# Three token-major projection groups of 512, 512 and 420 columns in place of four, with the index columns beside the chunked mixer

## The chip, the cores and the metric

The kernel runs on one core of a Trainium2 chip. The metric is the device time of the program on that core, in microseconds (us); lower is better.

## What is computed

Two layers of a decoder trunk with 512 tokens of width 1024. In each layer one input projection of the normalised tokens feeds four mixers of width 256, whose gated outputs are merged and projected back:

```
h = rmsnorm(x, g_pre)
proj = jnp.einsum('bsd,dc->bsc', h, w_in)
(a_q, a_k, a_v, a_iq, a_ik, a_iw, b_b, b_c, b_x, c_q, c_k, c_v,
 d_u, d_v, gate_paths, merge_logits) = _split_cols(proj, IN_SPLITS)
o_a = dsa_sparse_attention(rope(a_q), rope(a_k), a_v, rope(a_iq), rope(a_ik), a_iw)
o_b = short_gated_conv(b_b, b_c, b_x, conv_w, conv_b)
o_c = stick_breaking_attention(c_q, c_k, c_v)
o_d = chunked_spatial_gating(d_u, d_v, ln_g, ln_b, w_spatial, b_spatial)
z = jnp.einsum('bsnw,nwd->bsnd', stack(o_a, o_b, o_c, o_d) * silu(gate_paths), w_branch)
merged = jnp.sum(jax.nn.sigmoid(merge_logits + b_merge) * z, axis=2)
x = x + rmsnorm(merged @ w_out, g_post)
x = x + (p_i @ w_ple) * sigmoid(x @ w_ple_gate)
```

Mixer A picks, for each token, its 128 best earlier tokens by an index score (from the columns iq, ik and iw) and attends to those alone. Mixer C (stick-breaking attention) needs cq, ck and cv. Mixer D (chunked gating) normalises dv per token and mixes it inside chunks of 128 tokens.

## The kernel before

Every float32 product is made of three matmuls on TensorE (`mm3`, L267 to L271): both factors are split into a rounded half and the rest (names ending in h and l), and hh, hl and lh are summed in PSUM. A weight chunk of up to 128 x 1024 arrives by DMA as `raw`; `split_chunk` makes `wh` on ScalarE (L246) and `wl` on VectorE (L248). `cmm` uses `wh`, `wh`, `wl` as the stationary operands of the first three matmuls of a step, so `wl` is wanted by the third.

The order of work on all engines is written out by `step`, one call of which is a step of the plan here. A step emits, in this order: the ScalarE and VectorE work on results of earlier steps (`front`), the splits that are due, the work of the mixers (`back`), the selection of mixer A (`idle`); then the step's main matmuls; then any split that is due only after them (a late split); then short matmuls and transposes that the generators asked for with `yield PE`. Each engine runs its own list in that order, so what stands in one step's list on VectorE delays all that stands behind it.

In each layer the steps are: T1 (aq, ak; 512 columns, token-major), cq and ck in steps 4 to 7, CV (cv, 256 columns) in 8 and 9, T2 (av, iq, ik, iw; 420 columns) in 10 to 13, the convolution's six column steps in 14 to 19, du in 20 and 21, DV (dv, 256 columns) in 22 and 23, eight gate steps in 24 to 31 and 32 merge steps in 32 to 63. A column step or a T step has 24 matmuls; a merge step has 24 into `mg` and 6 into `z`. CV and DV go through `tpairs`: two token tiles of 256 columns share a PSUM bank and 48 matmuls make one step.

The selection (`select`, L840 and after) builds for tiles 1, 2 and 3 a score row `cur` of 256, 384 or 512 columns and then runs 16 rounds on VectorE: MAX8 finds the eight largest, MATCH_REPLACE8 strikes them out. `RATES` says how many rounds a step may emit: 1 from its start in the convolution steps, 2 from du on, 3 in the gate steps, 2 in the merge steps. In the merge steps a late split falls due in steps 35, 39, 43, 47, 51 and 55, for the first merge chunk of the very next step.

Of the kernel before, what the change touches and what calls it, by code (L numbers as in the profile page):

```python
# [12 lines left out]
F32R = mybir.dt.float32r  # L13
I32 = mybir.dt.int32
AF = mybir.ActivationFunctionType
ALU = mybir.AluOpType
# [4 lines left out]
P = 128  # L21
# [23 lines left out]
def _span(name, i=0, n=None):  # L45
    o, w = OFF[name]
    n = w if n is None else n
    return list(range(o + i, o + i + n))
# [4 lines left out]

TGROUPS = {
    "T1": _span("aq") + _span("ak"),
    "T2": _span("av") + _span("iq") + _span("ik") + _span("iw"),
    "CV": _span("cv"),
    "DV": _span("dv"),
}
CCOLS = {(n, c): _span(n, P * c, P) for n in ("cq", "ck", "bb", "bc", "bx", "du") for c in range(2)}  # L60
CCOLS.update({(f"gate{n}", c): _span("gate", W * n + P * c, P) for n in range(4) for c in range(2)})
# [1 line left out]

PAIRED = ("T1", "T2", "Y0", "Y1", "G0")


def tiles_of(cols):
# [3 lines left out]
def chunk_plan():  # L73

    plan, step = [], 0
    for l in range(L):
        here = []

        def tgroup(name, cols, steps):
            nonlocal step  # L80
            n = tiles_of(cols)
            for c in range(KT // n):
                first, last = step, step + steps - 1
                if name in PAIRED and (l, name) != (0, "T1"):
                    first, last = step + c // 2, step + c // 2 + 2
                here.append(("t", n * cols, (name, c), first, last))
            step += steps

        def ccols(*names):
            nonlocal step  # L90
            for a in names:
                here.append(("c", KT * P, a, step, step))
                step += 1

        def both(n):
            return [(n, 0), (n, 1)]

        tgroup("T1", 512, 4)
        ccols(*both("cq"), *both("ck"))
        tgroup("CV", 256, 2)  # L100
        tgroup("T2", 420, 4)
        for c in range(2):
            ccols(("bc", c), ("bx", c), ("bb", c))
        ccols(*both("du"))
        tgroup("DV", 256, 2)
        for n in MERGES:
            ccols(*both(f"gate{n}"))
        for n in MERGES:
            for h in range(2):
                here.append(("w", 1024, (n, h), step, step + 3))  # L110
                ccols(*((f"merge{n}", dt) for dt in range(4 * h, 4 * h + 4)))
        for h in range(2):
            tgroup(f"Y{h}", 512, 4)
        for h in range(2):
            here.append(("p", 1024, h, step, step))
            step += 1
            tgroup(f"G{h}", 512, 4)
        plan.append(here)
    return plan
# [34 lines left out]
QB, TB, SB, RAWB, WB, LEAD = 10, 25, 24, 3, 6, 4  # L154


STICKD, SELECT0, ATTEND0, RATES = 3, 8, 5, (1, 2, 3, 2)


START = ("s0 h0 t0 w e0 m00 s1 h1 w t1 m01 e1 s2 h2 m10,11 t2 w e2 s3 h3 m02,12,20,21 t3 w e3 "  # L160
# [20 lines left out]
def hybrid_kernel(ctx: ExitStack, tc: tile.TileContext, w, x, p_t, pos, inv_freq, rows, small, ws_t, b_sp, out):  # L181
# [12 lines left out]
    def T(name, shape=(P, 512), dt=F32):  # L194
        return tpool.tile(list(shape), dt, tag="t", name=name)
# [21 lines left out]
    def bank(name):  # L217
        return psum.tile([P, 512], F32, tag="ps", name=name)
# [40 lines left out]
    def take(n=1):  # L259
        k = state["use"]  # L260
        state["use"] += n
        for c in chunks[k:k + n]:
            assert c[3] <= state["step"] + n
        return list(range(k, k + n))
# [10 lines left out]
    def half_h(h, src, scale=None):  # L275
        if scale is None:
            A.copy(h, src)
        else:
            A.mul(h, src, scale)
# [35 lines left out]
    def step(mm=None):  # L315
        splits = list(due(False)) if mm else []
        if chained[0]:
            waiting = rounds(list(front))
            waiting += rounds(splits + back)
        else:  # L320
            waiting = rounds(front + splits + back)
        waiting += rounds(list(idle))
        if mm:
            mm()
            rounds(list(due(True)))
        while waiting:
            waiting = rounds(waiting)
        if mm:
            state["step"] += 1
# [143 lines left out]
    def heads(x):  # L473
        return x.rearrange("p (n f) -> p n f", n=4)
# [10 lines left out]
    def tmm(ps, lhs, ks, t, cols, n, kts=range(KT), cs=slice(0, 512)):  # L485
        for kt in kts:
            h, lo = halves[ks[kt // n]]
            s = slice(kt % n * cols + cs.start, kt % n * cols + min(cs.stop, cols))
            mm3(ps, lhs(kt, t), (h[:, s], lo[:, s]), kt == 0, kt == KT - 1)
# [26 lines left out]
            step(lambda: tmm(ps[:, :cols], lhs, ks, t, cols, n))  # L516
            front.append(use(t, ps))

    def tpairs(lhs, use):

        ks = take(2)
        for t in (0, 2):
            ps = bank("tp")

            def mm():
                for i in range(2):
                    tmm(ps[:, 256 * i:256 * i + 256], lhs, ks, t + i, 256, 4)

            step(mm)
            front.append(use(t, ps.rearrange("p (t f) -> p t f", t=2)))  # L530

    def ccol(use):

        k, = take()
# [76 lines left out]
    for l in range(L):  # L611
# [170 lines left out]
        sticks = [later(stick(c, b), STICKD * (2 * c + b)) for c in range(2) for b in range(2)]  # L782
        back.extend(sticks)

        def use_cv(t, ps):
            for i in range(2):
                half_h(vc[:, t + i, :, 0], heads(ps[:, i]))
            yield HOP
            for i in range(2):
                half_l(vc[:, t + i, :, 0], vc[:, t + i, :, 1], heads(ps[:, i]))  # L790

        tpairs(hlhs, use_cv)

        va = stacked("va")
        ikT = T("ikT", dt=F32R)

        def use_t2(t, ps):
            half_h(va[:, t, :, 0], heads(ps[:, 0:256]))
            iw = sm("iw", 4)
            V.tensor_scalar(iw, ps[:, 416:420], IDX_SCALE, None, op0=ALU.mult)  # L800
            iws[t] = iw
            r = T("ir")
            rope(r[:, :160], ps[:, 256:416], cos32, sin32, 5, t, "ropei")
            yield HOP
            half_l(va[:, t, :, 0], va[:, t, :, 1], heads(ps[:, 0:256]))

            sk = T("isk")[:, :P].rearrange("p (a b f) -> p a b f", a=2, b=2)
            rk = r[:, 128:160]
            rk2 = rk[:, None, :].to_broadcast([P, 2, 32])
            if t:  # L810
                sq = T("isq", (P, 4, 2, 2, 32))
                rq = r[:, :128].rearrange("p (h f) -> p h f", h=4)
                for a in range(2):
                    A.copy(sq[:, :, 0, a].bitcast(F32R), rq)
            for a in range(2):
                A.copy(sk[:, a, 0].bitcast(F32R), rk)
            yield HOP
            if t:
                for a in range(2):
                    V.tensor_tensor(sq[:, :, 1, a], rq, sq[:, :, 0, a], op=ALU.subtract)  # L820
            V.tensor_tensor(sk[:, :, 1], rk2, sk[:, :, 0], op=ALU.subtract)
            yield PE
            if t:
                tp = bank("iqtr")
                for h in range(4):
                    nc.tensor.transpose(tp[:, h * P:(h + 1) * P], sq[:, h].rearrange("p a b f -> p (a b f)"), ident)
            tk = bank("iktr")
            nc.tensor.transpose(tk[:, :P], sk.rearrange("p a b f -> p (a b f)"), ident)
            yield STEP
            if t:  # L830
                q = T("iqT", dt=F32R)
                A.copy(q, tp)
                iqT[t] = q
            V.tensor_copy(ikT[:, t * P:(t + 1) * P], tk[:, :P])

        tgroup(hlhs, 420, use_t2, 1)

        rate = {"select": 0}

        def select():  # L840

            bias[0] = bias0
            for i in range(1, NT):
                n = (i + 1) * P
                cur = T("cur")
                for h in range(4):
# [111 lines left out]
                yield STEP  # L958


        idle.append(later(select(), SELECT0))
        rate["select"] = RATES[0]
        cur = {}

        def use_bc(c, ps):
# [29 lines left out]
            A.copy(du[c], ps)  # L995
            yield STEP

        rate["select"] = RATES[1]
        for c in range(2):
            ccol(lambda ps, c=c: use_du(c, ps))  # L1000
        lnp = load(T("lnp"), bass.AP(tensor=rows.tensor, offset=rows.offset + l * 2560 + 2048, ap=[[0, P], [1, 512]]))
# [9 lines left out]
            yield HOP  # L1011
            yield from split(wsT[0], wsT[1], ws)

        def use_dv(t, ps):
            mv, r = sm("bag", 4), sm("lnr", 2)
            for i in range(2):
                st = sm("bst", 6)
                V.bn_stats(st, ps[:, i])
                V.bn_aggr(mv[:, 2 * i:2 * i + 2], st)
            yield from rstd(r, [mv.rearrange("p (t k) -> p t k", t=2)[:, :, 1]], 1)  # L1020
            yield HOP
            vf = T("vf", (P, 2, W))
            for i in range(2):
                V.tensor_scalar(vf[:, i], ps[:, i], mv[:, 2 * i:2 * i + 1], r[:, i:i + 1], op0=ALU.subtract, op1=ALU.mult)
            g, b = [lnp[:, W * i:W * i + W][:, None, :].to_broadcast([P, 2, W]) for i in range(2)]
            V.tensor_tensor(vf, vf, g, op=ALU.mult)
            V.tensor_tensor(vf, vf, b, op=ALU.add)
            yield HOP
            yield from split(vn[0][:, t:t + 2], vn[1][:, t:t + 2], vf)

        def mix():
            for c in range(2):
# [19 lines left out]
                raw[3, c] = o  # L1052

        back.append(prepare_ws())
        tpairs(hlhs, use_dv)
        back.append(later(mix(), 1))


        rate["select"] = RATES[2]

        def use_gate(n, c, ps):
            g = T("gate")
# [13 lines left out]
        for n in MERGES:  # L1076
            for c in range(2):
                ccol(lambda ps, n=n, c=c: use_gate(n, c, ps))
        rate["select"] = RATES[3]


        m, mT = {}, {}
# [219 lines left out]
```

## Time and profile before

| | |
|---|---|
| median of three runs | 1103.43 us (1102.41 to 1104.86) |
| the profiled execution | 1104.97 us |
| its span, first to last instruction | 1103.3 us |
| TensorE matmul (PE) | 1088.5 us busy, 99% |
| VectorE (DVE) | 771.8 us, 70% |
| ScalarE (ACT) | 492.3 us, 45% |
| GpSimd (POOL) | 23.0 us, 2% |
| mean granted TensorE clock | 0.997 |

The busy share of an engine is that of the whole span. TensorE is the engine that is never idle for long; another engine costs time where TensorE waits for it. Of the chain of work that ended last, the page of the profile puts 93% on TensorE and 4% on VectorE.

### The profile page before, as it was taken

What the parts mean: (1) busy time and instruction counts of PE and PEld (TensorE: products, weight loads), DVE (VectorE), ACT (ScalarE), POOL (GpSimd) and SP (SyncE); (2) the same over time, 40 slices, a digit from 0 to 9 for tenths busy, and PEclk for the clock granted to TensorE, in tenths of its full rate; (3) what the DMA queues carried; (4) which work ended last, traced back from release to release, by engine and by line L of the source; (5) the groups of instructions that cost most, each with busy time, mean ns of one, the idle gap of its engine ahead of it and who ended that gap; (6) DMA issues with size and microseconds to landing.
All of it is one profiled execution on the core that took longest, in us unless ns stands there. A gap on an engine that the chain in (4) does not pass through costs nothing.

```text
span 1103.3 us, 14018 instructions
## 1 busy us (share of the span) xinstructions
PE 1088.5 (99%) x5300; PEld 923.3 (84%) x5300; DVE 771.8 (70%) x1450; ACT 492.3 (45%) x857; POOL 23.0 (2%) x46
## 2 busy tenths in 40 slices
PE   7989999999999999999999999999999999999998
PEld 5879889888888888888788998988888888888887
DVE  5878778966888754446588688698678877554562
ACT  4557654324423533335436576534243254333351
POOL 2000001000000000000000000000000000000000
PEclk9989999999999999999999999999999999999999
DMA  5223232232323223552441322313222322336331
GB/s 193 78 82 96 76 99 79 80 93 77 96 93 97 73 82 98 177 164 86 143 133 52 108 77 77 101 58 115 77 96 77 97 75 77 96 96 226 99 115 38
DMA packets 34349, 109.01 MB, mean 99 GB/s; under 512 B 4057, under 2 KB 4841, under 8 KB 34282
## 3 DMA queue, kind: packets, MB, share of 16 engines
q1 hardware_dynamic: 34218, 108.10, 30.9%
q8 instruction: 41, 0.67, 0.3%
q14 instruction: 26, 0.21, 0.1%
q0 software_dynamic: 64, 0.03, 0.1%
HBM read 103.91 MB, written 4.19 MB: 98 GB/s over the span
## 4 chain that ended last, share of the span: by engine, by line
PE 93%; DVE 4%; DMA 1%; issue 1%; ACT 1%; SPq 0%; POOL 0%; DVEq 0%; ACTq 0%
PE mg L269 11%; PE mg L271 11%; PE mg L270 11%; PE tg L269 7%; PE tg L271 7%; PE tg L270 7%; PE cc L269 6%; PE cc L270 6%; PE cc L271 6%; PE z L270 3%; PE z L269 3%; PE z L271 3%; PE tp L270 2%; PE tp L271 1%; PE tp L269 1%; PE cs L721 1%
## 5 line engine op out<-in xcount | busy, mean ns | idle before, releaser
L248 DVE TENSOR_TENSOR wl<-raw,wh 128x1024 fp32r<-128x1024 f32 (+1 forms) x180 | 217.2, 1211 | 19.7 <-ACT wh L246 19.0
L269 PE MATMUL mg<-hh,wh 128*128 128x512 f32 x512 | 199.7, 390 | 0.0
L271 PE MATMUL mg<-hh,wl 128*128 128x512 f32 x512 | 199.4, 389 | 0.0
L270 PE MATMUL mg<-hl,wh 128*128 128x512 f32 x512 | 199.3, 389 | 0.0
L246 ACT CAST wh<-raw 128x1024 fp32r<-128x1024 f32 (+1 forms) x180 | 185.5, 1039 | 10.9 <-DMA raw<-in_w 4.3
L1089 ACT ACTIVATE g<-mg,prm 128x512 f32<-128x512 f32 x64 | 44.1, 690 | 227.6 <-PE mg L271 227.6
L269 PE MATMUL cc<-hh,wh 128*128 128x512 f32 x320 | 125.4, 392 | 0.0
L271 PE MATMUL cc<-hh,wl 128*128 128x512 f32 x320 | 124.9, 390 | 0.0
L270 PE MATMUL cc<-hl,wh 128*128 128x512 f32 x320 | 124.8, 390 | 0.0
L271 PEld LDWEIGHTS mg<-hh,wl 128*128 128x128 f32 x512 | 96.1, 188 | 20.3
L270 PEld LDWEIGHTS mg<-hl,wh 128*128 128x128 f32 x512 | 96.2, 188 | 19.7
L269 PEld LDWEIGHTS mg<-hh,wh 128*128 128x128 f32 x512 | 96.1, 188 | 19.6
L1095 DVE SCALAR_TENSOR_TENSOR g<-g,z 128x512 f32<-128x512 f32 x48 | 32.9, 686 | 72.1 <-PE z L271 72.0
L271 PEld LDWEIGHTS cc<-hh,wl 128*128 128x128 f32 x320 | 60.1, 188 | 13.0 <-DVE wl L248 0.3
L270 PEld LDWEIGHTS cc<-hl,wh 128*128 128x128 f32 x320 | 60.2, 188 | 11.7
L269 PEld LDWEIGHTS cc<-hh,wh 128*128 128x128 f32 x320 | 60.1, 188 | 11.6
L869 DVE MAX8 m<-cur 128x8 f32<-128x256 f32 (+2 forms) x96 | 53.6, 559 | 4.4 <-POOL cur L861 2.6
L870 DVE MATCH_REPLACE8 cur<-m,cur 128x256 f32<-128x256 f32 (+2 forms) x96 | 52.1, 542 | 0.0
L269 PE MATMUL tg<-wh,xh 128*128 128x512 f32 (+1 forms) x136 | 51.8, 381 | 0.0
L271 PE MATMUL tg<-wh,xl 128*128 128x512 f32 (+1 forms) x136 | 51.3, 377 | 0.0
L270 PE MATMUL tg<-wl,xh 128*128 128x512 f32 (+1 forms) x136 | 51.2, 377 | 0.0
L269 PE MATMUL tg<-wh,mh 128*128 128x512 f32 x128 | 50.0, 390 | 0.0
(249 smaller groups left out, 2027.6 us busy)
## 6 DMA issues: line engine op xcount, KB each, us to landing
raw<-in_w SPq DMA_DIRECT2D x172, 512.0 KB, 3.6
raw<-in_w SPq DMA_DIRECT2D x8, 420.0 KB, 3.2
x<-in_x SPq DMA_DIRECT2D x8, 256.0 KB, 6.9
res<-in_x SPq DMA_DIRECT2D x8, 256.0 KB, 4.5
xdram<-res SPq DMA_DIRECT2D x8, 256.0 KB, 3.3
res<-xdram SPq DMA_DIRECT2D x8, 256.0 KB, 5.7
out<-res SPq DMA_DIRECT2D x7, 256.0 KB, 2.2
gpost<-in_rows SPq DMA_DIRECT2D x2, 512.0 KB, 5.4
```

The source lines that it names most:

```text
L246: A.copy(h[:, :n], r[:, :n])
L248: V.tensor_tensor(lo[:, :n], r[:, :n], h[:, :n].bitcast(F32), op=ALU.subtract)
L269: nc.tensor.matmul(ps, ah, bh, start=start, stop=False)
L270: nc.tensor.matmul(ps, ah, bl, start=False, stop=False)
L271: nc.tensor.matmul(ps, al, bh, start=False, stop=stop)
L721: nc.tensor.matmul(ps[:, (i - first) * P:], tri if i == own else ones, sh[u][q][:, ci:ci + S - i * P], start=(i == blocks[0] and q == 0), ...
L869: V.max(m8, cur[:, :n])
L870: V.match_replace(cur[:, :n], m8, cur[:, :n], TAKEN)
L1089: A.activation(g, ps, AF.Tanh, bias=b_merge(n, dt), scale=0.5)
L1095: V.scalar_tensor_tensor(g, g, 1.0, z, op0=ALU.add, op1=ALU.mult)
```

## The change

The projections become T1 (512), T2 (av and cv, 512) in steps 8 to 11, and T3 (dv, iq, ik, iw, 420) in steps 20 to 23; the convolution moves to steps 12 to 17 and du to 18 and 19. `tpairs` goes. The work on the index columns (rope, split, transposes) and the normalisation of dv are now both in `use_t3`, per token tile. The selection starts after T3 and runs 3 rounds in a step, in gate steps and merge steps alike; before it starts a tile it waits until that tile's index queries are there. The mixing of D starts two steps later than it did after its projection.

```
 TGROUPS = {
     "T1": _span("aq") + _span("ak"),
-    "T2": _span("av") + _span("iq") + _span("ik") + _span("iw"),
-    "CV": _span("cv"),
-    "DV": _span("dv"),
+    "T2": _span("av") + _span("cv"),
+    "T3": _span("dv") + _span("iq") + _span("ik") + _span("iw"),
 }
-PAIRED = ("T1", "T2", "Y0", "Y1", "G0")
+PAIRED = ("T1", "T2", "T3", "Y0", "Y1", "G0")
...
-STICKD, SELECT0, ATTEND0, RATES = 3, 8, 5, (1, 2, 3, 2)
+STICKD, MIX0, SELECT0, ATTEND0, RATES = 3, 3, 1, 5, (3, 3)
...
+        def use_t2(t, ps):
+            for k, v in enumerate((vc, va)):
+                half_h(v[:, t, :, 0], heads(ps[:, 256 - 256 * k:512 - 256 * k]))
+            yield HOP
+            for k, v in enumerate((vc, va)):
+                half_l(v[:, t, :, 0], v[:, t, :, 1], heads(ps[:, 256 - 256 * k:512 - 256 * k]))
+        tgroup(hlhs, 512, use_t2, 1)
...
             for i in range(1, NT):
+                while i not in iqT:
+                    yield STEP
...
+        def use_t3(t, ps):
+            mv, r, st = sm("bag", 2), sm("lnr", 1), sm("bst", 6)
+            V.bn_stats(st, ps[:, 0:W])
+            V.bn_aggr(mv, st)
+            yield from rstd(r, [mv[:, 1:2]], 1)
+            iw = sm("iw", 4)
+            V.tensor_scalar(iw, ps[:, 416:420], IDX_SCALE, None, op0=ALU.mult)
+            iws[t] = iw
+            ir = T("ir")
+            rope(ir[:, :160], ps[:, 256:416], cos32, sin32, 5, t, "ropei")
+            yield HOP
...
+            vf = T("vf")[:, :W]
+            V.tensor_scalar(vf, ps[:, 0:W], mv[:, 0:1], r, op0=ALU.subtract, op1=ALU.mult)
+            V.tensor_tensor(vf, vf, lnp[:, 0:W], op=ALU.mult)
+            V.tensor_tensor(vf, vf, lnp[:, W:2 * W], op=ALU.add)
+            yield HOP
+            if t:
+                for a in range(2):
+                    V.tensor_tensor(sq[:, :, 1, a], rq, sq[:, :, 0, a], op=ALU.subtract)
+            V.tensor_tensor(sk[:, :, 1], rk2, sk[:, :, 0], op=ALU.subtract)
+            half_h(vn[0][:, t], vf)
+            yield PE
...
-        tpairs(hlhs, use_dv)
-        back.append(later(mix(), 1))
-        rate["select"] = RATES[2]
+        tgroup(hlhs, 420, use_t3, 1)
+        back.append(later(mix(), MIX0))
+        idle.append(later(select(), SELECT0))
+        rate["select"] = RATES[0]
...
-        rate["select"] = RATES[3]
+        rate["select"] = RATES[1]
```

What this does to the order on VectorE shows at two places. The first is the end of a token tile's work on the index columns, in layer 0 (tile 2 of T2 before, of T3 after; L634 to L639 and L619 to L624 are the rope, `isq` and `isk` feed the transposes that TensorE runs behind the step's main matmuls). Before:

```order
L834 CAST ikT<-iktr 128x128
L800 TENSOR_SCALAR iw<-tg 128x4
L634 TENSOR_TENSOR ir<-tg,cos_124 128x160
L638 TENSOR_TENSOR ropei<-tg,sin_125 128x5x16 x2
L639 TENSOR_TENSOR ir<-ir,ropei 128x160
L756 TENSOR_TENSOR cz<-cz,cs 128x384
L736 TENSOR_TENSOR cz<-cz,far_129 128x512
L283 TENSOR_TENSOR va<-tg,va 128x4x64
L248 TENSOR_TENSOR wl_1115<-raw_890,wh_1114 128x1024
L820 TENSOR_TENSOR isq<-ir,isq 128x4x32 x2
L821 TENSOR_TENSOR isk<-ir,isk 128x2x32
```

After, in the first gate step:

```order
L1003 CAST ikT<-iktr 128x128
L960 BN_STATS bst<-tg 128x6
L961 BN_AGGR bag<-bst 128x2
L439 TENSOR_SCALAR lnr<-bag 128x1
L964 TENSOR_SCALAR iw<-tg 128x4
L619 TENSOR_TENSOR ir<-tg,cos_124 128x160
L623 TENSOR_TENSOR ropei<-tg,sin_125 128x5x16 x2
L624 TENSOR_TENSOR ir<-ir,ropei 128x160
L246 TENSOR_TENSOR wl_1696<-raw_1495,wh_1695 128x1024
L760 TENSOR_TENSOR oc<-cav,oc 64x512
L981 TENSOR_SCALAR vf<-tg,bag,lnr 128x256
L982 TENSOR_TENSOR vf<-vf,lnp 128x256
```

The statistics now stand ahead of the rope, and the three `vf` operations (the third, L983, follows the last row shown) between the weight's rest and `isq`.

The second place is a merge step with a late split, step 43 of layer 0 (`g` and `m` are the merge of the step before, `wl` a weight's rest; the second `wl` is the late one, for step 44). Before:

```order
L1095 SCALAR_TENSOR_TENSOR g<-g,z 128x512
L1096 TENSOR_TENSOR m_2411<-m_2411,g 128x512
L248 TENSOR_TENSOR wl_2948<-raw_2737,wh_2947 128x1024
L869 MAX m_2955<-cur 128x8
L870 MATCH_REPLACE cur<-m_2955,cur 128x512
L869 MAX m_2958<-cur 128x8
L870 MATCH_REPLACE cur<-m_2958,cur 128x512
L248 TENSOR_TENSOR wl_2992<-raw_2821,wh_2991 128x1024
```

After:

```order
L1070 SCALAR_TENSOR_TENSOR g<-g,z 128x512
L1071 TENSOR_TENSOR m_2306<-m_2306,g 128x512
L246 TENSOR_TENSOR wl_2855<-raw_2654,wh_2854 128x1024
L804 SCALAR_TENSOR_TENSOR cur<-relu,iw,cur 128x512
L804 SCALAR_TENSOR_TENSOR cur<-relu,iw,cur 128x512
L814 MAX m_2871<-cur 128x8
L815 MATCH_REPLACE cur<-m_2871,cur 128x512
L814 MAX m_2874<-cur 128x8
L815 MATCH_REPLACE cur<-m_2874,cur 128x512
L814 MAX m_2877<-cur 128x8
L815 MATCH_REPLACE cur<-m_2877,cur 128x512
L246 TENSOR_TENSOR wl_2911<-raw_2738,wh_2910 128x1024
```

The late `wl` has three rounds ahead of it in place of two, and in this step the end of the score row for tile 3 as well, which before stood in step 42.

## Rows read from the trace of the kernel before

**Rows 1.** The page: busy time, share of the span and instructions of each engine.

```profile
PE 1088.5 (99%) x5300; PEld 923.3 (84%) x5300; DVE 771.8 (70%) x1450; ACT 492.3 (45%) x857; POOL 23.0 (2%) x46
```

**Rows 2.** Windows: us, then PE, PEld, DVE, ACT, POOL busy (instructions), PEclk, DMA, GB/s.

```profile
63.45:67.50 4.05, 0.28 (x2) 0.00 (x0) 3.96 (x7) 3.33 (x4) 0.00 (x0) 0.83 0.00 0
67.50:72.90 5.40, 5.39 (x24) 5.35 (x25) 5.00 (x6) 0.00 (x0) 0.00 (x0) 0.50 0.49 159
...
548.00:552.00 4.00, 2.92 (x18) 2.25 (x17) 3.27 (x6) 2.54 (x5) 0.55 (x1) 1.00 0.03 5
```

**Rows 3.** Timeline of PE (start, us, engine, line, operation): first and last matmuls of runs.

```profile
82.27 0.35 PE L269 MATMUL tg<-wh,hh 128*128 128x420 f32 x1
...
86.67 0.35 PE L271 MATMUL tg<-wh,hl 128*128 128x420 f32 x1
...
573.83 0.39 PE L270 MATMUL tg<-wl,hh 128*128 128x512 f32 x1
...
580.17 0.40 PE L271 MATMUL tg<-wh,hl 128*128 128x512 f32 x1
...
703.73 0.28 PE L271 MATMUL tp<-wh,hl 128*128 128x256 f32 x1
...
708.41 0.28 PE L271 MATMUL tp<-wh,hl 128*128 128x256 f32 x1
```

**Rows 4.** Timeline of DVE, merge step 43.

```profile
305.29 0.69 DVE L1095 SCALAR_TENSOR_TENSOR g<-g,z 128x512 f32<-128x512 f32 x1 [1.32 <-PE z L271]
...
307.75 0.69 DVE L869 MAX8 m<-cur 128x8 f32<-128x512 f32 x1
...
310.66 1.22 DVE L248 TENSOR_TENSOR wl<-raw,wh 128x1024 fp32r<-128x1024 f32 x1
```

**Rows 5.** Timeline of PEld (weight loads), the first `wl` load of step 44.

```profile
312.04 0.19 PEld L271 LDWEIGHTS mg<-hh,wl 128*128 128x128 f32 x1
```

**Rows 6.** Timeline of DVE, merge step 42.

```profile
296.44 0.69 DVE L1095 SCALAR_TENSOR_TENSOR g<-g,z 128x512 f32<-128x512 f32 x1
...
300.97 0.69 DVE L869 MAX8 m<-cur 128x8 f32<-128x512 f32 x1 [0.45 <-POOL cur L861]
```

**Rows 7.** Timeline, step 39's late `wl` on DVE and its weight load on PEld.

```profile
279.12 1.22 DVE L248 TENSOR_TENSOR wl<-raw,wh 128x1024 fp32r<-128x1024 f32 x1
...
281.05 0.19 PEld L271 LDWEIGHTS mg<-hh,wl 128*128 128x128 f32 x1
```

**Rows 8.** Timeline, end of T2: the index transposes on PE, DVE behind them.

```profile
112.94 0.27 PE L828 MATMUL iktr<-ident,isk 128*128 128x128 f32 x1
113.25 0.29 DVE L834 CAST ikT<-iktr 128x128 fp32r<-128x128 f32 x1
```

**Rows 9.** Timeline of DVE in the fourth T2 step, token tile 1.

```profile
99.10 0.28 DVE L834 CAST ikT<-iktr 128x128 fp32r<-128x128 f32 x1
99.30 0.15 DVE L800 TENSOR_SCALAR iw<-tg 128x4 f32<-128x4 f32 x1
...
100.26 0.55 DVE L756 TENSOR_TENSOR cz<-cz,cs 128x384 f32<-128x384 f32 x1
...
101.52 1.22 DVE L248 TENSOR_TENSOR wl<-raw,wh 128x1024 fp32r<-128x1024 f32 x1
102.65 0.49 DVE L820 TENSOR_TENSOR isq<-ir,isq 128x128 f32<-128x128 f32 x2
```

**Rows 10.** Timeline of DVE behind DV's first pair: statistics, then `vf`.

```profile
169.72 0.40 DVE L1018 BATCH_NORM_STATS2 bst<-tp 128x6 f32<-128x256 f32 x1
...
170.45 0.55 DVE L756 TENSOR_TENSOR cz<-cz,cs 128x384 f32<-128x384 f32 x1
...
172.05 0.99 DVE L1024 TENSOR_SCALAR vf<-tp,bag,lnr 128x256 f32<-128x256 f32 x2
```

**Rows 11.** Timeline of ACT, the first gate.

```profile
183.82 1.28 ACT L1063 ACT_TABLE_LOAD   x1
185.12 0.60 ACT L1063 ACTIVATE gate<-cc 128x512 f32<-128x512 f32 x1
```

More of the change, by code (lines that the diff above doesn't have):

```diff
@@ L99, in chunk_plan @@
         ccols(*both("cq"), *both("ck"))
-        tgroup("CV", 256, 2)
-        tgroup("T2", 420, 4)
+        tgroup("T2", 512, 4)
         for c in range(2):
@@ L104, in chunk_plan @@
         ccols(*both("du"))
-        tgroup("DV", 256, 2)
+        tgroup("T3", 420, 4)
         for n in MERGES:
@@ L517, in tgroup @@
             front.append(use(t, ps))
[L519 to L530, printed above, removed]
     def ccol(use):
@@ L783, in hybrid_kernel @@
         back.extend(sticks)
-        def use_cv(t, ps):
-            for i in range(2):
-                half_h(vc[:, t + i, :, 0], heads(ps[:, i]))
+        va = stacked("va")
+        def use_t2(t, ps):
+            for k, v in enumerate((vc, va)):
+                half_h(v[:, t, :, 0], heads(ps[:, 256 - 256 * k:512 - 256 * k]))
             yield HOP
-            for i in range(2):
-                half_l(vc[:, t + i, :, 0], vc[:, t + i, :, 1], heads(ps[:, i]))
-        tpairs(hlhs, use_cv)
@@ L794, in hybrid_kernel @@
[L794 to L834, printed above, removed]
@@ L836, in hybrid_kernel @@
-        tgroup(hlhs, 420, use_t2, 1)
+            for k, v in enumerate((vc, va)):
+                half_l(v[:, t, :, 0], v[:, t, :, 1], heads(ps[:, 256 - 256 * k:512 - 256 * k]))
+        tgroup(hlhs, 512, use_t2, 1)
         rate = {"select": 0}
@@ L958, in attend @@
                 yield STEP
-        idle.append(later(select(), SELECT0))
-        rate["select"] = RATES[0]
         cur = {}
@@ L996, in use_du @@
             yield STEP
-        rate["select"] = RATES[1]
         for c in range(2):
@@ L1012, in prepare_ws @@
             yield from split(wsT[0], wsT[1], ws)
[L1014 to L1020, printed above, removed]
-            yield HOP
[L1022 to L1027, printed above, removed]
-            yield HOP
-            yield from split(vn[0][:, t:t + 2], vn[1][:, t:t + 2], vf)
+        ikT = T("ikT", dt=F32R)
@@ new lines, in use_t3 @@
+        def use_t3(t, ps):
[8 more added lines that the diff above has]
+            rope(ir[:, :160], ps[:, 256:416], cos32, sin32, 5, t, "ropei")
+            yield HOP
+            sk = T("isk")[:, :P].rearrange("p (a b f) -> p a b f", a=2, b=2)
+            rk = ir[:, 128:160]
+            rk2 = rk[:, None, :].to_broadcast([P, 2, 32])
+            if t:
+                sq = T("isq", (P, 4, 2, 2, 32))
+                rq = ir[:, :128].rearrange("p (h f) -> p h f", h=4)
+                for a in range(2):
+                    A.copy(sq[:, :, 0, a].bitcast(F32R), rq)
+            for a in range(2):
+                A.copy(sk[:, a, 0].bitcast(F32R), rk)
+            vf = T("vf")[:, :W]
+            V.tensor_scalar(vf, ps[:, 0:W], mv[:, 0:1], r, op0=ALU.subtract, op1=ALU.mult)
+            V.tensor_tensor(vf, vf, lnp[:, 0:W], op=ALU.mult)
+            V.tensor_tensor(vf, vf, lnp[:, W:2 * W], op=ALU.add)
+            yield HOP
+            if t:
+                for a in range(2):
+                    V.tensor_tensor(sq[:, :, 1, a], rq, sq[:, :, 0, a], op=ALU.subtract)
+            V.tensor_tensor(sk[:, :, 1], rk2, sk[:, :, 0], op=ALU.subtract)
+            half_h(vn[0][:, t], vf)
+            yield PE
+            if t:
+                tp = bank("iqtr")
+                for h in range(4):
+                    nc.tensor.transpose(tp[:, h * P:(h + 1) * P], sq[:, h].rearrange("p a b f -> p (a b f)"), ident)
+            tk = bank("iktr")
+            nc.tensor.transpose(tk[:, :P], sk.rearrange("p a b f -> p (a b f)"), ident)
+            yield STEP
+            half_l(vn[0][:, t], vn[1][:, t], vf)
+            if t:
+                q = T("iqT", dt=F32R)
+                A.copy(q, tp)
+                iqT[t] = q
+            V.tensor_copy(ikT[:, t * P:(t + 1) * P], tk[:, :P])
```

## Prediction, made before the changed kernel ran

> **What bounds the kernel now.** I read the page first: TensorE is busy for 99% of the span and VectorE for 70% [rows 1]. So time is saved by taking work off TensorE, and lost wherever TensorE is made to wait. Next I read the windows for the places where it waits today. The only large one is at the start, where PE does 0.28 us of work in 4.05 us while VectorE is busy for 3.96 of them [rows 2]. The timeline of VectorE was read last, step by step, for how late its results are when TensorE wants them. The reader is to see that at two places of this change, the merge steps with a late split and the end of the index columns, the room is smaller than the share of 70% suggests.
>
> **What TensorE saves.** A pair of 256-column matmuls becomes one of 512. From its starts, the 256-column matmul is issued every 0.120 us (39 intervals from 703.73 to 708.41), the 512-column one every 0.2264 us (28 from 573.83 to 580.17), the 420-column one every 0.1913 us (23 from 82.27 to 86.67) [rows 3]. A layer had 96 of 256 for CV, 96 of 256 for DV and 96 of 420; it gets 96 of 512 and 96 of 420. That saves 96 x (0.240 - 0.2264) = 1.3 us a layer, 2.6 us in both. The first 24 of CV's matmuls ran at half clock behind the stall at the start, 24 of them in 5.40 us at a granted clock of 0.50, which is 1.2 GHz [rows 2], so for the twelve pairs there I count nothing: 2.4 us in all. Bounds: 2.0 and 2.6.
>
> The Trainium skill, TensorE: Matmul & The Clock Gate, section "Wait — 56ns, not 53.3ns?", speaks against this term: start to start a warm matmul takes its columns at 2.4 GHz and a fixed 2.5 ns. By that rule joining two saves only those 2.5 ns, an estimated 0.5 us for both layers, and the sum below would come out 1.9 us higher. The rows disagree with the rule at both widths (0.120 and 0.2264 us against 0.109 and 0.216), and I go by the rows.
>
> **What costs nothing.** The chunks are as many and hold the same columns. The order of VectorE up to the second weight rest that step 8 wants is the same, so the wait at the start stays. The convolution, moved two steps ahead, loses the index work that stood beside it; before, that region ran without a gap, so lighter VectorE steps gain nothing there. On POOL there are eight small powers in both layers instead of four wider ones; their result is wanted only after the weight's rest, at least 2 us later. The loads for the mixer D on SP's queue come two steps earlier, behind the same kind of release. ScalarE splits the same bytes. If VectorE lags in the last gate steps (its list there is 6 to 8 us for a step of 5.4), the cover is that a weight's rest is made two or three steps ahead of its use; that cover fails only where a split is late, and these are costed next.
>
> **The merge steps.** A merge step is 30 matmuls, 6.8 us on TensorE [rows 3]. In step 43, VectorE's list from the merge to the first round takes 2.46 us, two rounds 2.91 us (1.46 each), and the late `wl` then runs from 310.66 to 311.88 [rows 4]. TensorE loads that `wl` at 312.04 [rows 5]. So the room is 0.16 us, and a third round, 1.46 us, doesn't fit.
>
> - *Step 47* has nothing but the merge, a split, three rounds and the late split. The list is 2.46 + 3 x 1.46 = 6.84 us, as long as the step itself, so VectorE doesn't catch up between two late splits, and step 48's `wl` comes 1.46 - 0.16 = 1.3 us late. I take 1.3; bounds 0.9 and 1.9.
> - *Step 43* also gets the end of the score row. The row's end stood in step 42 before, without a late split: from the merge to the first round 4.53 us [rows 6], against 2.46 [rows 4]. That is 2.1 us more, on top of the round: 2.1 + 1.5 - 0.16 = 3.4 us; but two score matmuls of 512 columns (0.45 us) now run on TensorE between the end of the merge's operands and step 43's matmuls, which gives room. I take 3.0; bounds 2.4 and 3.4.
> - *Step 39*: the late `wl` ended at 280.34 and was loaded at 281.05, 0.7 us of room [rows 7]. A round of 384 columns is somewhat shorter than 1.46, about 1.25; the bias operation that stood there (about 0.3) moves on: 1.25 - 0.3 - 0.7 = 0.3 us. Bounds 0 and 0.8.
> - *Step 35* is to the 384-column row what step 43 is to the 512-column one, but has no early split in it (a `wl` of 1.2 us less) and shorter rounds and score operations: 3.0 - 1.2 - 3 x 0.2 - 0.5 = about 0.6; I take 0.5. Bounds 0 and 1.0.
>
> Together 5.1 us a layer, 10.2 in both; bounds 6.6 and 14.2. At steps 51 and 55 the selection is over, so nothing changes there.
>
> **The end of T3.** Behind the main matmuls of steps 23, 24 and 25 TensorE wants work of VectorE (the weights of mixer C behind 23, `isq` for the transposes behind 24 and 25). VectorE's list hangs on the previous step's transposes: `ikT` starts 0.31 us after `iktr` [rows 8], then `ikT` takes 0.20, `iw` and the rope 0.96, a `wl` 1.13, the two `isq` together about 0.4 [rows 9]. New in this list are the statistics, 0.73 us for one tile [rows 10], and `vf`: one subtraction of 0.5 us (half of the pair [rows 10]) and two operations that I take at 0.45 each, nearest to the 0.40 of the statistics on the same 256 columns, 1.4 in all.
>
> - *Step 23*, 24 x 0.1913 + 0.1 = 4.7 us on TensorE: 0.31 + 0.20 + 0.73 + 0.5 (`cz`) + 0.96 + 1.13 + 1.4 + 0.5 (`cwl`) = 5.7, late by 1.0.
> - *Step 24*, 24 x 0.2264 + 0.1 = 5.5 us: without `cz` and `cwl`, with `oc` (0.6) and `isq` (0.4): 5.7, late by 0.2.
> - *Step 25*, 5.5 us: the gate waits for ScalarE, which copies `iqT` (512 columns like the gate, so 0.6), loads a table (1.28) and runs the gate (0.60) [rows 11] before it starts on `wh` (1.0, no longer than the `wl`): 3.6 us until `wl` can start, then 1.13 + 1.4 + 0.4 = 6.5, late by 1.0.
>
> Together 2.2 us a layer, 4.4 in both. Bounds: 0.8 a layer, if only half of one wait shows, and 3.6, if every dependent operation has 0.1 us more ahead of it.
>
> **The sum.** -2.4 + 10.2 + 4.4 = +12.2 us. The durations are from one execution of 1104.97 us (span 1103.3 and 1.7 around it), which lies 1.5 above the median of the runs, 1103.43; the sum is added to the median: 1115.6 us. With all lower bounds -2.6 + 6.6 + 1.6 = +5.6, with all upper -2.0 + 14.2 + 7.2 = +19.4.
>
> **The rivals.**
>
> - *Faster: the waits stay hidden and only the saving shows.* The mechanism is that a late split finishes before TensorE loads it, in step 43 above all. It decides at 0.16 us of room [rows 4, 5]: VectorE would have to start the step's merge over 1.3 us earlier, or overlap its rounds. For it speaks that other, unlisted waits could already slow VectorE in the trace of before; against it that from 305.29 to 311.88 VectorE has no gap in it. 1103.4 - 2.4 = 1101.0 us. Chance 0.07.
> - *Only the end of T3 waits*, the merges being hidden: 1101.0 + 4.4 = 1105.4. Chance 0.06.
> - *Only the merges wait*, the index work being in time: 1101.0 + 10.2 = 1111.2. Chance 0.12.
> - *The clock falls.* Behind the idle 3.8 us at the start, TensorE was granted 0.50 for 5.40 us, which cost 2.7 us; behind an idle 1.1 us at 548 to 552 it kept 1.00 [rows 2]. The wait of 3.0 us in step 43 lies between these and nearer to the first, but it's the only one so long. If the clock falls once in each layer: 1115.6 + 5.4 = 1121.0. Chance 0.17. The Trainium skill, TensorE: Matmul & The Clock Gate, section "What's actually happening", has the same: a gate sets the rate by how busy the array has been of late, and half rate is the default. By that rule the fall is possible here; the trace agrees in its one case.
> - *The change doesn't do what it says*: two matmuls of 256 cost no more than one of 512. Then +14.6, 1118.0, inside the range; it's not given a chance of its own.
>
> **How the numbers follow.** The forecast, 1115.6 us, has the remaining chance, 0.58. The range of 8 in 10 goes from 1106 to 1122: it leaves out the fully hidden case (0.07), most of the case with T3 alone (0.06) and the forecast's own upper end. A measurement of this kernel can tell 0.2%, 2.2 us, from no change. Faster by that is the first rival, 0.07; within it is the half of the second, with the smallest sums of the others, 0.05; slower is the rest, 0.88.
>
> **What would show it.** In the profile after: `wl` on VectorE as what TensorE waited for, some 2 to 3 us once a layer at the start of step 44 and 1 to 2 at step 48; `cwl` and `isq` as releasers of about 1 us each behind steps 23 and 25; no 256-column projection matmuls. Wrong would be a TensorE with no idle in the merges, or idle time that ends with a DMA.

## The result and the profile after

The changed kernel takes 1119.03 us (median of 4 runs, 1117.95 to 1124.1) against 1104.14 us for the kernel before beside it (1102.41 to 1105.33): a ratio of 1.0145, 95% interval 1.0111 to 1.0179. It is slower by 14.9 us. Three of the four runs lie between 1117.95 and 1119.27 us, at mean granted clocks of 0.994 to 0.996; the fourth took 1124.1 us at 0.992. The profiled execution took 1119.27 us, its span is 1117.5 us, 14.2 more than that of before.

The page of the changed kernel (busy us, share of the span, instructions) answers to [rows 1]:

```profile
span 1117.5 us, 13637 instructions
PE 1091.0 (98%) x5108; PEld 912.1 (82%) x5108; DVE 773.3 (69%) x1466; ACT 494.5 (44%) x861; POOL 21.6 (2%) x50
```

TensorE has 192 instructions fewer and is busy for 2.5 us more. The waits of TensorE over the whole span (who waited for whom: us in total, times, longest) show what it now waits for. The 3.7 us for `tg` belong to the start and were there before (3.8 us); `mg` (a merge's matmuls), `iqtr` (the index transposes) and `cav` (a product of mixer C, which needs the rest `cwl`) are new:

```profile
PE mg L269 <- DVE wl L246: 7.7, 4, 2.6
PE tg L268 <- DVE wl L246: 4.0, 2, 3.7
PE iqtr L994 <- DVE isk L988: 3.1, 4, 1.1
...
PE cav L478 <- DVE cwl L281: 1.7, 2, 0.8
```

They stand where the prediction put them: `cav` behind step 23, `iqtr` behind steps 24 and 25, `mg` at the start of steps 44 and 48, the same in both layers. VectorE in step 43 (timeline: start, us, engine, line, operation) answers to [rows 4, 6]:

```profile
310.31 0.69 DVE L814 MAX8 m<-cur 128x8 f32<-128x512 f32 x1 [0.46 <-POOL cur L806]
...
313.34 0.69 DVE L814 MAX8 m<-cur 128x8 f32<-128x512 f32 x1
...
314.74 1.22 DVE L246 TENSOR_TENSOR wl<-raw,wh 128x1024 fp32r<-128x1024 f32 x1
```

Three rounds follow the end of the score row, from 310.31 on, 1.5 us each, and the late `wl` begins at 314.74. On the clock of the span that is 4.1 us later than before; 0.9 us of it is that TensorE itself begins step 43 later (305.95 for 305.01). TensorE, over the same stretch:

```profile
312.98 0.39 PE L268 MATMUL mg<-hl,wh 128*128 128x512 f32 x1
316.01 0.49 PE L269 MATMUL mg<-hh,wl 128*128 128x512 f32 x1 [2.65 <-DVE wl L246]
...
317.34 0.63 PE L267 MATMUL mg<-hh,wh 128*128 128x512 f32 x1
317.77 0.63 PE L268 MATMUL mg<-hl,wh 128*128 128x512 f32 x1
...
320.45 0.39 PE L269 MATMUL mg<-hh,wl 128*128 128x512 f32 x1
```

The second matmul of step 44 is issued at 312.98, the third, which needs that `wl`, at 316.01. Behind it the matmuls come 0.43 us apart (317.34 to 317.77) in place of the 0.23 of [rows 3]. The windows (us, busy of PE, PEld, DVE, ACT, POOL, then the granted clock) tell why; they answer to [rows 2]:

```profile
313.00:316.00 3.00, 0.36 (x2) 0.00 (x0) 2.93 (x6) 0.22 (x1) 0.00 (x0) 1.00 0.00 0
...
318.00:320.00 2.00, 2.00 (x6) 1.51 (x6) 1.93 (x5) 0.00 (x0) 0.00 (x0) 0.50 0.73 213
320.00:324.00 4.00, 4.00 (x19) 3.31 (x18) 2.75 (x6) 1.06 (x2) 0.00 (x0) 0.99 0.28 114
...
346.00:350.00 4.00, 3.68 (x16) 3.10 (x17) 3.93 (x7) 0.00 (x0) 0.00 (x0) 1.00 0.54 148
...
863.00:866.00 3.00, 3.00 (x7) 2.44 (x8) 2.93 (x5) 0.00 (x0) 0.00 (x0) 0.50 0.55 171
```

Behind the wait of 2.65 us the granted clock fell to 0.50, the lower of its two levels, 1.2 GHz, and came back by 320; behind the wait of 1.21 us at step 48 it stayed at 1.00. In layer 1 the same happened: 2.64 us of wait, then 0.50 (the last row), and no fall behind step 48's 1.20 us.

### The profile page after: what moved, and what is told of

It is laid out like the page before. It is cut to its first block, busy times and chain, and to the rows that moved or that the text cites. A ratio compares the mean times of both kernels' runs of the same rounds, so it can differ in the third digit from the quotient of the medians.

```text
span 1117.5 us, 13637 instructions
## 1 busy us (share of the span) xinstructions
PE 1091.0 (98%) x5108; PEld 912.1 (82%) x5108; DVE 773.3 (69%) x1466; ACT 494.5 (44%) x861; POOL 21.6 (2%) x50
## 4 chain that ended last, share of the span: by engine, by line
PE 86%; DVE 9%; issue 2%; ACT 2%; DMA 1%; POOL 0%; SPq 0%; DVEq 0%; POOLq 0%; ACTq 0%
PE mg L269 10%; PE mg L267 10%; PE mg L268 10%; PE tg L268 8%; PE tg L269 8%; PE tg L267 8%; PE cc L267 5%; PE cc L268 5%; PE cc L269 5%; DVE wl L246 2%; PE z L269 2%; PE z L267 2%; PE z L268 2%; PE cs L706 1%; PE ptr L888 1%
## 5 line engine op out<-in xcount | busy, mean ns | idle before, releaser
L269 PE MATMUL mg<-hh,wl 128*128 128x512 f32 x512 | 201.7, 394 | 7.7 <-DVE wl L246 7.7
L1064 ACT ACTIVATE g<-mg,prm 128x512 f32<-128x512 f32 x64 | 44.1, 690 | 237.6 <-PE mg L269 227.1
L268 PE MATMUL tg<-wl,hh 128*128 128x512 f32 (+1 forms) x192 | 74.0, 385 | 4.0 <-DVE wl L246 4.0
L267 PE MATMUL tg<-wh,hh 128*128 128x512 f32 (+1 forms) x192 | 74.7, 389 | 1.4 <-ACT hh L275 1.4
L269 PE MATMUL tg<-wh,hl 128*128 128x512 f32 (+1 forms) x192 | 73.7, 384 | 0.0
```

The lines of the kernel that those rows point to most:

```text
L267: nc.tensor.matmul(ps, ah, bh, start=start, stop=False)
L268: nc.tensor.matmul(ps, ah, bl, start=False, stop=False)
L269: nc.tensor.matmul(ps, al, bh, start=False, stop=stop)
L1064: A.activation(g, ps, AF.Tanh, bias=b_merge(n, dt), scale=0.5)
```

## The experiments

Theory W is the prediction's: TensorE waits because of what stands ahead of a few results in VectorE's list, at the late weight rests and at the end of T3. Each ratio is against the kernel before on the same chip. Differences in us are between medians taken on different chips, where the kernel before had medians of 1103.2 to 1104.1 us, so a difference of less than 1 us tells nothing.

### 2 rounds in all merge steps

```
-(3, 3)
+(3, 2)
```

> The changed kernel with the rate of the merge steps put back to 2 rounds (RATES 3, 2); nothing else. Theory W (the late weight rests cost what the third round puts ahead of them): the waits at steps 44 and 48, their slow clock and the traces of waits at 36 and 40, about 6.1 us a layer, go. But the selection now ends in step 52 in place of 48, so the attention of tiles 2 and 3 runs from step 53 to 58, and the last merge group waits for it from step 56 on: two or three steps without main matmuls, 3 to 5 us each. Net 1119.0 - 12.3 + 2 x (6 to 15) = 1119 to 1137 us. Rival R (what counts is how much selection a step holds in all): fewer rounds in a step simply give the time back, 1107 us.

Measured: 1125.89 us, ratio 1.0203 (1.0187 to 1.022). The `mg` waits are gone, and the run is still slower than the change. TensorE's waits, and the place of the largest of the new ones in its timeline (`av` is the attention's product with the values; it needs `ptl`, the rest of the transposed weights of the attention):

```profile
PE av L478 <- DVE ptl L281: 7.7, 2, 3.8
```

```profile
402.79 0.28 PE L477 MATMUL av<-pth,va 128*128 128x256 f32 x1
406.90 0.38 PE L478 MATMUL av<-ptl,va 128*128 128x256 f32 x1 [3.83 <-DVE ptl L281]
...
412.15 0.73 PE L267 MATMUL mg<-hh,wh 128*128 128x512 f32 x1
```

From 402.79 to 412.15 there are only the attention's short matmuls: the last merge group waits for the attention, as expected, and behind the wait the clock falls to 0.50. So the rate of 3 was not free to choose. The selection starts later in the changed kernel, and at 2 rounds it ends too late. Rival R falls.

### 2 rounds in the steps with a late split, 3 in the others

```
-if done >= rate["select"]:
+if done >= rate["select"] - ((state["step"], True) in when):
```

> The changed kernel with 3 rounds in every step but those with a late split (35, 39, 43, 47), which get 2; the selection still ends in step 48. Theory W: the wait at step 48 (1.2 us) goes, the one at 44 falls from 2.65 to about 1.2 us, and with so short a wait TensorE keeps its full clock there, which gives back another 1.6 us: 4.3 us a layer, 1119.0 - 8.6 = 1110.4 us, and TensorE's granted clock behind step 44's wait stays at 1.00. Rival R (the number of rounds doesn't matter, VectorE is simply behind): under 2 us in all, 1117 us or more. Rival C (the clock falls for another reason than the length of the wait): the granted clock still falls to 0.50 there, 1113.6 us.

Measured: 1109.7 us, ratio 1.0063 (1.0048 to 1.0078), 0.7 us from the forecast of W. Of the `mg` waits one a layer is left, 1.1 us, and the clock behind it (same windows as above, at this kernel's times) stays up:

```profile
PE mg L269 <- DVE wl L246: 2.3, 2, 1.1
```

```profile
313.20:314.30 1.10, 0.00 (x0) 0.00 (x0) 1.10 (x2) 0.00 (x0) 0.00 (x0) 1.00 0.00 0
314.30:316.00 1.70, 1.68 (x7) 1.42 (x8) 1.67 (x3) 0.00 (x0) 0.00 (x0) 1.00 0.15 24
```

One round less in each of four steps of a layer, with the same total of rounds (steps 40 and 48 take three in place of one), gives back 9.3 us. The wait, not the amount of selection, is what costs: rival R falls. The clock stayed up behind the short wait, which speaks against rival C; that the length of the wait alone decides is not shown, and the run with `vf` behind the index work speaks against it.

### Late splits ahead of the rounds

```
-    waiting += rounds(list(idle))
-    if mm:
-        mm()
-        rounds(list(due(True)))
+    if mm:
+        rounds(list(due(True)))
+    waiting += rounds(list(idle))
+    if mm:
+        mm()
```

> The changed kernel with the late splits of each step issued ahead of that step's selection rounds in place of behind its matmuls; still 3 rounds a step, the same amount of work on VectorE. Theory W (it is the place in VectorE's queue, not the amount of work): all merge waits and the slow clock behind them go, 6.1 us a layer, 1119.0 - 12.3 = 1106.7 us, and what is left over the kernel before are the waits at the end of T3. Rival R (VectorE's list with three rounds is as long as a step and has no room for a second split): the lateness moves to the next step's weight rests or to the merges' results, and less than half comes back, 1113 us or more.

Measured: 1110.53 us, ratio 1.0069 (1.0054 to 1.0084). No `mg` wait is left at any step, with three rounds everywhere: it is the place in VectorE's queue. But 8.5 us came back, not 12.3. In the trace 7.7 us of waits are gone, and of the `mg` matmuls themselves 4.5 us, which is slow clock and the slower first matmuls behind each wait (called restarts here). Added up by their starts, the `av` matmuls of the attention and its transposes `ptr` took 1.6 us more than before, since VectorE comes out of the selection late; and T2's matmuls of layer 0 took 1.0 us more than in the changed kernel, without their waits, since the clock of 0.50 behind the wait at the start lasted 6.8 us in this execution and 3.4 in the other. Some of the rest lies in waits at the start and at the change of layers. So rival R is right in a small part.

### vf behind the index work

A `yield HOP` hands on to the next generator within the same step.

```
-            vf = T("vf")[:, :W]
-            V.tensor_scalar(vf, ps[:, 0:W], mv[:, 0:1], r, op0=ALU.subtract, op1=ALU.mult)
-            V.tensor_tensor(vf, vf, lnp[:, 0:W], op=ALU.mult)
-            V.tensor_tensor(vf, vf, lnp[:, W:2 * W], op=ALU.add)
             yield HOP
...
             V.tensor_tensor(sk[:, :, 1], rk2, sk[:, :, 0], op=ALU.subtract)
+            vf = T("vf")[:, :W]
+            V.tensor_scalar(vf, ps[:, 0:W], mv[:, 0:1], r, op0=ALU.subtract, op1=ALU.mult)
+            V.tensor_tensor(vf, vf, lnp[:, 0:W], op=ALU.mult)
+            V.tensor_tensor(vf, vf, lnp[:, W:2 * W], op=ALU.add)
             half_h(vn[0][:, t], vf)
```

> The changed kernel with the three vf operations of T3 issued behind isq and isk in place of ahead of them (and so behind cwl too). Theory W: 1.4 us leave the chain in front of what TensorE waits for, so the waits behind steps 23 (0.83 us), 24 (0.48) and 25 (1.09) all go or fall under 0.1 us: 2.4 us a layer and about 0.3 of restarts, 1119.0 - 5.2 = 1113.8 us. Rival T (ScalarE's table load and gate set the wait behind step 25, and the statistics the others): only half of it goes, 1116.5 us.

Measured: 1114.93 us, ratio 1.0117 (1.0095 to 1.014), 4.1 us better than the change. The wait behind step 23 is gone, that behind 24 fell from 0.48 to 0.31 and that behind 25 from 1.09 to 0.77. ScalarE and VectorE ahead of the transposes of step 25 (timelines) tell what sets the last:

```profile
179.90 0.59 ACT L1001 CAST iqT<-iqtr 128x512 fp32r<-128x512 f32 x1
180.49 1.28 ACT L1038 ACT_TABLE_LOAD   x1
181.78 0.60 ACT L1038 ACTIVATE gate<-cc 128x512 f32<-128x512 f32 x1
182.28 1.04 ACT L244 CAST wh<-raw 128x1024 fp32r<-128x1024 f32 x1
183.22 0.49 ACT L977 CAST isq<-ir 128x128 fp32r<-128x128 f32 x2
```

```profile
182.41 0.69 DVE L1045 TENSOR_TENSOR gate<-gate,bt 128x512 f32<-128x512 f32 x1 [0.19 <-ACT gate L1038]
183.35 1.22 DVE L246 TENSOR_TENSOR wl<-raw,wh 128x1024 fp32r<-128x1024 f32 x1 [0.24 <-ACT wh L244]
184.49 0.48 DVE L983 TENSOR_TENSOR isq<-ir,isq 128x128 f32<-128x128 f32 x2
```

`isq` on VectorE stands behind the gate's product, which waits for the table load and the gate, and behind `wl`, which waits for `wh`. Rival T holds for this step.

The 4.1 us are not all owed to the moved operations. In layer 0 of this execution step 44 waited as long as in the changed kernel, and the granted clock stayed at 1.00 behind it (timeline of TensorE, then windows); in layer 1, behind 2.64 us, it fell to 0.50:

```profile
313.84 0.50 PE L269 MATMUL mg<-hh,wl 128*128 128x512 f32 x1 [2.65 <-DVE wl L246]
```

```profile
313.80:316.00 2.20, 2.16 (x9) 1.80 (x10) 2.17 (x3) 0.00 (x0) 0.00 (x0) 1.00 0.54 97
316.00:320.00 4.00, 4.00 (x19) 3.31 (x18) 3.83 (x10) 0.83 (x2) 0.00 (x0) 1.00 0.60 209
```

With one fall in place of two, the `mg` matmuls without their waits took 352.4 us here and 353.8 in the changed kernel, 1.5 us less. That leaves an estimated 2.6 us for the edit, as in the trace, where 2.7 us of waits went; it is what rival T had for the whole (2.5 us).

### The index work first

The new order of `use_t3`, the lines that moved:

```
             rope(ir[:, :160], ps[:, 256:416], cos32, sin32, 5, t, "ropei")
+            if t:
...
+                    A.copy(sq[:, :, 0, a].bitcast(F32R), rq)
+            for a in range(2):
+                A.copy(sk[:, a, 0].bitcast(F32R), rk)
             yield HOP
+            if t:
+                for a in range(2):
+                    V.tensor_tensor(sq[:, :, 1, a], rq, sq[:, :, 0, a], op=ALU.subtract)
+            V.tensor_tensor(sk[:, :, 1], rk2, sk[:, :, 0], op=ALU.subtract)
...
+            V.bn_stats(st, ps[:, 0:W])
+            V.bn_aggr(mv, st)
+            yield from rstd(r, [mv[:, 1:2]], 1)
+            yield HOP
+            yield HOP
...
+            V.tensor_scalar(vf, ps[:, 0:W], mv[:, 0:1], r, op0=ALU.subtract, op1=ALU.mult)
```

> The changed kernel with T3's work in another order: rope, then the copies of isq and isk on ScalarE ahead of the weight split, the table load and the gate, then isq and isk on VectorE, and only then the statistics and vf. Theory W with what the last runs showed (behind step 25 isq waits for ScalarE, which loads the gate's table first): the waits behind steps 24 and 25 go, that behind 23 falls to 0.3 us at most. 2.1 us a layer and the restarts, 1119.0 - 4.8 = 1114.2 us, with no iqtr among what TensorE waits for. Rival T (the index transposes wait for ikT of the step before, so the chain only shifts): no better than with vf alone behind the index work, 1114.9 us, with iqtr waits left.

Measured: 1114.45 us, ratio 1.0101 (1.0087 to 1.0114), 0.25 us from the forecast. No `iqtr` is left among what TensorE waits for, and of `cav` 0.14 us a layer; the four `mg` waits, and the clock's fall in both layers, are as in the changed kernel:

```profile
PE mg L269 <- DVE wl L246: 7.7, 4, 2.6
```

So the end of T3 cost 4.6 us, and it was the order inside `use_t3`, not the work that it holds. Rival T, in the form that the chain only shifts, falls.

### The kernel before with 3 rounds in a merge step

```
-(1, 2, 3, 2)
+(1, 2, 3, 3)
```

> The kernel before with 3 rounds in a merge step in place of 2 and nothing else of the change (its four projection groups stay). Theory W: the late weight rest in step 43 again has three rounds ahead of it, and here the attention of tiles 0 and 1 as well, which leaves VectorE behind by some us; so TensorE waits at step 44 for 1.3 us or more in each layer, and perhaps for attention results before it. 1103.2 + 2 x (1.3 to 4) = 1106 to 1111 us. Rival G (the waits in the merges come from the new grouping, which starts the selection later, and not from the rate): within 1 us of 1103.2.

Measured: 1118.36 us, ratio 1.0129 (1.0113 to 1.0144). The rate alone makes the kernel before as slow as the change did, so rival G falls; W's range was too low. TensorE's waits and VectorE's list before step 44 in this run:

```profile
PE mg L271 <- DVE wl L248: 9.2, 2, 4.6
PE av L480 <- DVE ptl L283: 0.7, 2, 0.4
```

```profile
297.35 0.69 DVE L869 MAX8 m<-cur 128x8 f32<-128x512 f32 x1
...
301.78 0.68 DVE L1095 SCALAR_TENSOR_TENSOR g<-g,z 128x512 f32<-128x512 f32 x1
...
308.66 0.68 DVE L1095 SCALAR_TENSOR_TENSOR g<-g,z 128x512 f32<-128x512 f32 x1
...
315.54 1.22 DVE L248 TENSOR_TENSOR wl<-raw,wh 128x1024 fp32r<-128x1024 f32 x1
```

VectorE is over 3 us behind before step 43 begins: the attention of tiles 0 and 1 shares steps 40 and 41 with the rounds, and from then on it works without a gap, one list every 6.88 us (301.78 to 308.66), as long as a step (6.80 us). The third round takes away the slack in which it caught up, so what it lost in step 41 it still lacks in step 44, on top of the round itself: 4.6 us.

### The kernel before with its late splits first

The edit is that of the third experiment.

> The kernel before with its late splits issued ahead of the selection rounds. A control: at 2 rounds the late rest came in time by 0.16 us, so TensorE has nothing to win: 1103.2 us, within 1.5. If it were faster by 2 us or more, part of what the next runs win would not be owed to the new grouping.

Measured: 1104.41 us, ratio 1.0003 (0.9994 to 1.0013). No difference, as expected of a control.

### All three repairs, and step 45

The first of these has the index work first, the late splits ahead of the rounds and 2 rounds in the steps with a late split.

> The changed kernel with the index work first, the late splits ahead of the rounds and 2 rounds in the steps with a late split. Theory W: all waits of the merges and nearly all at the end of T3 are gone, and what is left is the saving of the joined matmuls, 2.4 us, less 0.6 for what remains behind step 23 and some restarts: 1103.2 - 1.8 = 1101.4 us, 1100 to 1103.5. Rival S (the saving is given back elsewhere, in the gate steps that now hold the index transposes and the start of the selection): 1104 us or more, with TensorE busy and not waiting.

Measured: 1103.99 us, ratio 1.0003 (0.9994 to 1.0012). All waits of the change are gone but 0.14 us a layer behind step 23, and there is no gain over the kernel before that can be measured. W's 1101.4 us was missed, and its range too; the time is rival S's. S put the loss in the gate steps; the last run looks for it in the attention.

```
-((state["step"], True) in when)
+((state["step"], True) in when or state["step"] % 82 == 45)
```

> The kernel with all three repairs and, in addition, 2 rounds in merge step 45 too, so that the selection ends one step later (49). Theory L (with the waits gone, VectorE still enters the attention of tiles 2 and 3 about 0.8 us behind, since three rounds leave it no slack, and TensorE waits for ptl and pr there, 0.85 us a layer): the list of step 45 gets 1.4 us shorter, the lag is gone by step 49, and the av and ptr matmuls take 0.7 us a layer less: 1104.0 - 1.7 = 1102.3 us, faster than the kernel before by about 0.15%. Rival (that wait is set by ScalarE's exponentials or the transposes, not by VectorE's lag): no change against the run with all three, 1104.0 us.

Measured: 1101.86 us (12 runs), ratio 0.9978 (0.9969 to 0.9987). This is the fastest of all, below both kernels. In the run with all three repairs the first attention step of tiles 2 and 3 was late (timeline of TensorE):

```profile
350.84 0.28 PE L478 MATMUL av<-pth,va 128*128 128x256 f32 x1
351.26 0.39 PE L479 MATMUL av<-ptl,va 128*128 128x256 f32 x1 [0.15 <-DVE ptl L281]
...
351.79 1.27 PE L889 MATMUL ptr<-ident,pr 128*128 128x128 f32 x7
352.82 0.42 PE L901 MATMUL lg<-kT,qT 128*128 128x384 f32 x1
```

Seven transposes take 1.03 us there (351.79 to 352.82), against 0.71 us in the later units. With step 45 lightened the `av` and `ptr` matmuls, added up by their starts over both layers, fall from 19.9 to 18.1 us, which is the value before, where theory L had 1.4 us for the 1.8; the waits over 0.2 us that are left are those of the start and of the change of layers:

```profile
PE tg L268 <- DVE wl L246: 4.1, 2, 3.7
PE gpre L358 <- DMA line<-in_rows: 2.4, 1, 2.4
...
PE htr L454 <- DVE h L1228: 0.6, 1, 0.6
```

## Why the prediction was right

The forecast was +12.2 us, 1115.6, with a range of 1106 to 1122; measured were +14.9 us, 1119.0.

- **The saving of the joined matmuls**, put at 2.4 us. In layer 1, away from the start, the 192 matmuls of 256 columns and T1's 96 of 512 added up to 45.2 us by their starts (23.06 and 22.16); after, the 192 of 512 in T1 and T2 add up to 44.1: 1.15 us a layer, where 1.3 was taken. The rows decide against the rule of the Trainium skill, TensorE: Matmul & The Clock Gate, section "Wait — 56ns, not 53.3ns?", by which it would have been an estimated 0.24 us a layer; a joined pair saved 12 ns, not 2.5. With all waits mended and step 45 lightened, the kernel is 2.2 us below the one before, which agrees with this saving; in the traces layer 1, from T1's first matmul to the end, went from 540.2 to 539.5 us, and the larger part lies in layer 0 beside the start, so that all of it is the joined matmuls is not shown.
- **The end of T3**, put at 4.4 us (1.0, 0.2 and 1.0 a layer): 0.83, 0.48 and 1.09, so 4.8 us. The chain of step 23 ran as worked out: 5.36 us from `ikT` to the operation behind `cwl` (167.35 to 172.71), where the terms give 5.4. Step 24's was 0.3 longer. In step 25 the terms ahead of `wl` add up to 3.5 us and not to 3.6, which changes nothing. The index-first run won 4.6 us.
- **The merge steps**, put at 10.2 us, waited for 7.7. Step 43's wait was 2.65 us for 3.0 forecast, step 47's 1.21 for 1.3. Steps 35 and 39, put at 0.5 and 0.3 (step 35's terms add up to 0.7, not 0.6), were mis-sized: neither made a gap in the matmuls that the waits show, only the weight load came 0.2 to 0.3 us late, as that of step 40 shows:

```profile
282.10 0.19 PEld L269 LDWEIGHTS mg<-hh,wl 128*128 128x128 f32 x1 [0.27 <-DVE wl L246]
```

- **The clock** is the step that failed. I took it as staying up, with a chance of 0.17 that it falls. It fell behind both long waits, and that is what the sum lacks: the 1536 `mg` matmuls, added up by their starts and without the waits, took 353.8 us in the changed kernel, 352.4 in the run with one fall, 349.3 with the late splits first and 349.0 in the kernel before. So a fall cost about 1.5 us and the two 3 of the 4.8; the rest are restarts and the late loads of steps 36 and 40. I had put the falls at 5.4 from the one case at the start. Forecast and rival together are +17.6; the waits in the merges were 2.5 us shorter, and the falls with the restarts 0.6 cheaper, the end of T3 0.4 dearer, which comes to the measured +14.9. That it does so to the tenth is luck: the restarts at the end of T3 and the differences at the start, about 1 us each, are not in it. It is luck too that the forecast came as near as 2.7 us, since waits taken too long stood in for a clock taken as staying up. The Trainium skill, TensorE: Matmul & The Clock Gate, section "What's actually happening", says that the rate follows how busy the array has been of late; the traces agree in so far as every fall in the merges stands behind an idle stretch of TensorE, of 2.63 us or more.
- **What was said to cost nothing** cost nothing. The waits at the start (3.7 us) are in every run. VectorE's lag in the gate steps made no wait.

What is open: what decides whether the clock falls. It stayed up behind every wait of 1.1 and 1.2 us in the merges and fell behind those of 3.8 and 4.6. Behind 2.6 us it fell in both layers of the changed kernel and of the index-first run, and in layer 1 of the run with `vf` behind the index work, but not in that run's layer 0. So the length of the wait alone does not decide, and the time of one and the same kernel may differ by a fall; that is not shown, since one execution of each has a trace. The startup differs by about a microsecond from run to run, and the share of it in single differences under 1 us can't be told.

## What to carry to other kernels

An engine that is 70% busy over the span can have no room at all in the step that matters: compare, step by step, when a result is ready and when it's wanted, and look above all at what stands ahead of it in an in-order queue. Here one more round of work that nobody waits for yet, put ahead of weight rests of which one had 0.16 us to spare (and there with the end of a score row), cost some 12 us with the slow clock behind the wait; moving the rest ahead of the rounds took all of these waits away. When two pieces of work are joined for a small gain, order the joined work by who is waited for soonest, and give a queue that runs full for several steps a lighter one before the next result that is due.

## What was not expected

- A wait of TensorE of 2.65 us can lower its granted clock to 0.50, here for 3.4 us (316.7 to 320.1), which cost about 1.5 us more than the wait itself; once in six such waits of three traces it did not. Waits of 1.1 and 1.2 us left it at 1.00.
- A third round in the merge steps of the kernel before made a wait of 4.6 us, three times the round, because the lag of the attention steps before it no longer got worked off.
- The largest gain of a single edit over the changed kernel, 9.3 us, came from moving one round out of each of four steps a layer, without a round less in all.
